# Splitting the first product of a recurrent mixer into uneven parts of k tiles

## The chip, the cores and the metric

The kernel runs on one core of one Trainium2 chip. The metric is the device time in microseconds (us) of one execution. Engines are named as the profile names them: PE is TensorE's matmul, PEld its weight load, DVE is VectorE, ACT is ScalarE, POOL is GpSimd, and SP is SyncE, which issues the loads.

## The reference

256 tokens of width 1024 pass through two blocks. The first has a mixer of gated linear attention (GLA) and retention, and then a mixture of 32 experts with 2 chosen per token. The second has an HGRN2 mixer, a convolutional feed-forward net, a latent attention and a second net. The change lies in the HGRN2 mixer and reaches back into the experts ahead of it:

```
def _hgrn2_mixer(h, w_in, lower_bound, out_norm, w_out):
    q, f, i, g = jnp.split(h @ w_in, 4, axis=-1)          # w_in: 1024 x 4096
    forget = lb + (1.0 - lb) * jax.nn.sigmoid(f)
    key_in, log_f = 1.0 - forget, jnp.log(forget)
    o = _chunk_gated_recurrence(heads(jax.nn.silu(q)), heads(key_in), heads(i), heads(log_f))   # 8 heads of 128
    o = _rmsnorm_2(o, out_norm) * jax.nn.silu(heads(g))
    return o.reshape(B, S, D_MODEL) @ w_out
```

Everything is float32. Ahead of the mixer stand the experts' second product (hidden times `wd`, weighted and summed into the residual) and two norms in a row.

## The kernel before, in words

SBUF beside the constants is a pool of 21 equal tiles "S" of 128 x 2048 words. A weight chunk is one load of 1 MiB into one such tile. `add` puts the chunks into one stream, in which they are loaded in order by SP; `prefetch` issues as many loads as a plan, made from a dry run of the same program, says will fit. A chunk that a float32 product needs with full precision is split by `split` into a high and a low part (4 ACT copies into `wh`, 4 DVE subtractions into `wl`, two more S tiles), and `mm3` makes one product of three matmuls of those parts. `get` also splits the chunk that follows. The framework's scheduler puts the instructions of each engine into a fixed order from the program's order and a model of costs; each engine then runs its own list in that order. PSUM has 8 banks.

The experts' second product (in `moe`) runs over 64 blocks i: each takes a chunk `ex_d` of 1 MiB, makes 32 small matmuls into a bank `y` (L1165), ACT copies the bank (L1169), and 2 matmuls with `ct` sum it into `cb` (L1177). Eight blocks fill one k tile (128 of 1024 features) of the mixer's input, so `hgrn_tile(k)` comes at block i = 8k + 9 and transposes and scales that tile (L1320).

The mixer's first product is 1024 x 4096: 8 k tiles times 8 groups of 512 columns. Groups 0 and 2 are the forget gates f of heads 0 to 3 and 4 to 7, groups 1 and 3 the queries q, 4 and 5 the values, 6 and 7 the output gates. It is done in four parts p of two k tiles each (2p, 2p + 1), a part being 4 chunks `hg_in` of two groups. Parts 0 to 2 are "fillers": generators that `tick` advances by one step of one k tile and one group (12 matmuls of 256 columns or 6 of 512) behind each block. Part 0 is queued at tile 1, so its ticks run in blocks 17 to 32; part 1 in 33 to 48; part 2 from 49 to the end. Sums over the parts are kept in four S tiles `hsum`, one for two groups: part 0 is copied there by ACT (L1381), parts 1 and 2 are added by DVE (L1383). The chunks of parts 0 to 2 stand in the stream before `ex_d` chunks 12, 16, 20, ... 56, and their `split` is called at those blocks.

Part 3 (k tiles 6 and 7) runs in `hgrn`, after the experts. There the sum of the earlier parts first enters the PSUM bank by a matmul with the identity (L1356), then 24 more matmuls follow, and the result is read straight from PSUM: for f and q by a multiplication with the norm's row (L1440, DVE), for values and gates by an activation with the norm's column as scale (L1456, ACT). The norm's scale comes from the filler `close` (POOL L448, row by L506).

For each half c (4 heads), `prep(c)` turns f and q into decays and keys, then `decay_levels` runs seven doubling steps of DVE multiplications (L575, L576, L578) and small PE products (L546 `sc`, L553 to L562 `sd`); it holds four banks `sc` until step 16 and two banks `sd` until the scores are read. `decay_scores` sums six levels per head by matmuls with the identity (L604, `cd`), masks them (L611) and copies the far parts; `decay_out` multiplies by the values (L633 to L635), takes the norm over each head, and scales. `gate(c)` multiplies by the gates (L1503) and transposes (L520). `out_proj` then has two halves: the first needs `gate(0)`, the second `gate(1)`.

The order before: chunk 12 (f and q of half 0), `prep(0)`, then chunks 13 (f and q of half 1), 14 (values), 15 (gates) with the filler `chains` at one tick per k tile and group (six steps of half 0's levels, then both halves in turn); `prep(1)` comes behind chunk 13; `decay_out` of half 1 is queued behind all that as a filler of `out_proj`, four ticks per chunk.

`decay_scores` is called three times: once for the GLA mixer of the first block and twice here.

Of the kernel before, what the change touches and what calls it, by code (L numbers as in the profile page):

```python
# [19 lines left out]
P = 128  # L20
T = 256
D = 1024
# [71 lines left out]
def _layout(z):  # L94
# [9 lines left out]
    def pairs(a):  # L104
# [20 lines left out]
    out["hg_in"] = np.ascontiguousarray(  # L125
        hw.reshape(4, 2, P, 4, 2, 512).transpose(0, 3, 2, 4, 1, 5).reshape(16, P, 2048))
# [34 lines left out]


# [61 lines left out]
class Kern:  # L224
# [371 lines left out]
    def decay_scores(self, sc):  # L596

        nc = self.nc
        bm = self.c("bmask").rearrange("p (b i) -> p b i", b=4)[:, None].to_broadcast([P, 2, 4, 32])
        cd = self.bank("cd")  # L600
        for h in range(4):
            tv = sc["tm"][:, h * 384:(h + 1) * 384].rearrange("p (t l i) -> p t l i", t=2, l=6)
            for l in range(6):
                nc.tensor.matmul(cd[:, h * 64:(h + 1) * 64].rearrange("p (t i) -> p t i", t=2), self.ident, tv[:, :, l],  # L604
                                 start=h == 0 and l == 0, stop=h == 3 and l == 5)
        yield
        for h in range(4):
            st = sc["st"][:, h * 384:(h + 1) * 384]
            stv = st.rearrange("p (t i) -> p t i", t=3)
            b2 = sc["b2"][h // 2][:, h % 2 * 256:(h % 2 + 1) * 256]  # L610
            nc.vector.tensor_mul(stv[:, 0:3:2].rearrange("p t (b i) -> p t b i", b=4),  # L611
                                 cd[:, h * 64:(h + 1) * 64].rearrange("p (t i) -> p t i", t=2)[:, :, None, :]
                                 .to_broadcast([P, 2, 4, 32]), bm)
            nc.scalar.copy(st[:, 128:256], b2[:, 0:128])
            for t in range(2):
                d = st[:, 256 * t:256 * t + 128]
                nc.scalar.copy(d[0:64, 64:128], b2[64 * t:64 * t + 64, 128:192])
                for b in range(2):
                    nc.scalar.copy(d[64 * b:64 * b + 32, 64 * b + 32:64 * b + 64],
                                   b2[64 * b + 32 * t:64 * b + 32 * t + 32, 192:224])  # L620
            yield
# [53 lines left out]
    def setup(self):  # L675
# [22 lines left out]
        for r in range(16):  # L698
            if 3 <= r < 15:
                self.add(("hg_in", r - 3), A["hg_in"][r - 3], True)  # L700
            for i in range(4 * r, 4 * r + 4):
                self.add(("ed", i), A["ex_d"][i], False)
# [303 lines left out]
    def moe(self):  # L1006
# [149 lines left out]
        for i in range(64 + 2):  # L1156
            if i < 64:
                if i % 4 == 0 and 12 <= i < 60:
                    self.split(("hg_in", i // 4 - 3))
# [155 lines left out]
    def hgrn_tile(self, k):  # L1315

        nc, x, n = self.nc, self.x, self.hn
        b = self.bank("tp")
        for t in range(2):
            nc.tensor.transpose(b[:, t * P:(t + 1) * P], x[:, t * D + k * P:t * D + (k + 1) * P], self.ident)  # L1320
        self.high_low(b, self.hw[:, k:k + 1], n["h"], n["l"], k * T)
        if k % 2:
            self.fillers.append(self.hgrn_part(k // 2))
            if k < 7:
                self.hgrn_squares(k // 2)
# [16 lines left out]
    def hgrn_part(self, p, only=None, evict=None):  # L1342

        nc, n = self.nc, self.hn
        for s in range(4) if only is None else (only,):
            key = ("hg_in", 4 * p + s)
            h, l = self.get_split(key) if p < 3 else self.get(key)
            if p == 0:
                self.hsum[s] = self.S("hsum")
            for gi in range(2):  # L1350
                outs = [self.bank("gf") for _ in range(2)]
                sums = [self.hsum[s][:, o:o + 512] for o in ((gi * 1024, gi * 1024 + 512) if s < 2 else
                                                             (gi * 512, D + gi * 512))]
                if evict:
                    for a, b in zip(sums, outs):
                        nc.tensor.matmul(b, self.ident, a, start=True, stop=False)  # L1356
                for q in range(2):
                    o = (2 * p + q) * T
                    w = slice(gi * 1024 + q * 512, gi * 1024 + (q + 1) * 512)
                    first = q == 0 and not evict  # L1360
                    if s < 2:
                        xh, xl = n["h"][:, o:o + T], n["l"][:, o:o + T]
                        for ft in range(4):
                            a = slice(w.start + ft * P, w.start + (ft + 1) * P)
                            self.mm3(outs[ft // 2][:, (ft % 2) * T:(ft % 2 + 1) * T], h[:, a], l[:, a], xh, xl,
                                     first and ft % 2 == 0, q == 1 and ft % 2 == 1)
                    else:
                        for t in range(2):
                            a = slice(o + t * P, o + (t + 1) * P)
                            self.mm3(outs[t], n["h"][:, a], n["l"][:, a], h[:, w], l[:, w], first, q == 1)  # L1370
                    if q == 0:
                        yield
                if gi:
                    self.free(h, l)
                if evict:
                    evict(gi, sums, outs)
                    if gi and s < 2:
                        self.free(self.hsum[s])
                for a, b in zip(sums, outs):
                    if p == 0:  # L1380
                        nc.scalar.copy(a, b)  # L1381
                    elif p < 3:
# [3 lines left out]
    def hgrn(self):  # L1386
# [10 lines left out]
        self.fillers.pop()  # L1397
# [4 lines left out]

        def part(s, evict, ticks):
            for _ in self.hgrn_part(3, s, evict):
                self.tick(ticks)

        def close():
# [13 lines left out]
            yield  # L1421
# [5 lines left out]
            yield  # L1427
# [6 lines left out]
        def ev_row(dst):  # L1434
            def f(gi, sums, outs):
                if rowb is None:
                    late.append((f, (gi, sums, outs)))
                    return
                for i, o in enumerate(outs):
                    nc.vector.tensor_mul(e2(dst[gi][:, 1024 + i * 512:1536 + i * 512]), e2(o), rowb)  # L1440
            return f
# [10 lines left out]

        def ev_tok(func):
            def f(gi, sums, outs):
                for t, o in enumerate(outs):
                    nc.scalar.activation(sums[t], o, func, scale=rs[:, t:t + 1])  # L1456
            return f
# [13 lines left out]
        g = self.hsum[3]  # L1471
        self.fillers.append(close())
        part(0, ev_row((fr[0], kq[0])), 1)
        self.drain()
        prep(0, fr[0], kq[0])
# [11 lines left out]

        self.fillers.append(chains())
        part(1, ev_row((fr[1], kq[1])), 1)
        prep(1, fr[1], kq[1])  # L1490
        part(2, ev_tok(AF.Copy), 1)
        part(3, ev_tok(AF.Silu), 1)
# [3 lines left out]
        self.fillers.append(self.decay_out(sc[1], v, 4, P))  # L1496
# [376 lines left out]
```

## Time and profile before

| what | value |
|---|---|
| median of 3 runs | 1508.77 us (1504.38 to 1510.76) |
| the profiled execution, its own time | 1510.53 us |
| its span in the trace | 1508.5 us |
| PE busy | 1362.1 us, 90% of the span |
| DVE busy, ACT busy | 781.2 us, 649.4 us |
| loads | 368.31 MB on SP's queue |

All times in the rows below are microseconds from the start of the span. The own time holds 2.0 us that lie outside the span. A busy PE is a PE that has matmuls under way; they are pipelined, so a group "x48" with its total length tells more than the length of one record. A float32 matmul leaves two records in the trace.

### The profile page before, as it was taken

To read this page: it belongs to the slowest core of one execution; us is meant where nothing else is said; L and a number is where in the kernel's file an instruction comes from. 1 tells how busy PE (TensorE), PEld (TensorE's weight loads), DVE (VectorE), ACT (ScalarE), POOL (GpSimd) and SP (SyncE) were. 2 spreads that over 40 slices of the span, in tenths; PEclk is the share of its full clock that TensorE was granted. 3 is DMA by queue.
4 is the path that set the end of the run, shared out by engine and by line. 5 is a ranking of instruction groups with operands and counts; after the bars stand their busy time and mean duration, and the time that the engine had idled before them with its cause. 6 is when DMAs were issued, how large, how long until landed. Compare 5 with 4: busy or idle time off the path is not lost.

```text
span 1508.5 us, 28797 instructions
## 1 busy us (share of the span) xinstructions
PE 1362.1 (90%) x12062; PEld 1103.4 (73%) x12062; DVE 781.2 (52%) x1685; ACT 649.4 (43%) x1489; POOL 22.3 (1%) x25
## 2 busy tenths in 40 slices
PE   7999999999897666766699998889999998999998
PEld 6799878877763243324588876679999976899997
DVE  4876376645510020000124438548777767687794
ACT  5564535733310010000243326447566576565672
POOL 0000000000000000000000000000000010000000
PEclk9999999999898788768899999989999999999999
DMA  8353623485899999999999990536453215565400
GB/s 337 153 196 113 223 84 140 142 348 200 369 374 420 420 419 421 421 421 420 420 388 359 417 404 30 197 115 248 168 196 113 77 46 206 210 213 196 164 1 28
DMA packets 53544, 370.20 MB, mean 245 GB/s; under 512 B 6161, under 2 KB 7057, under 8 KB 9634
## 3 DMA queue, kind: packets, MB, share of 16 engines
q1 hardware_dynamic: 53410, 368.31, 62.3%
q8 instruction: 96, 1.57, 0.4%
q14 instruction: 38, 0.31, 0.1%
HBM read 367.24 MB, written 1.05 MB: 244 GB/s over the span
## 4 chain that ended last, share of the span: by engine, by line
PE 68%; DMA 22%; ACT 4%; DVE 4%; issue 1%; POOL 1%; SPq 0%; POOLq 0%; ACTq 0%; DVEq 0%
DMA w<-in_ex_gu 16%; PE u L370 6%; PE u L372 6%; PE u L371 6%; DMA w<-in_ex_d 5%; PE gt L371 5%; PE gt L372 5%; PE gt L370 5%; PE gf L370 3%; PE gf L371 3%; PE gf L372 3%; PE acc L371 3%; PE acc L370 3%; PE acc L372 3%; PE y L1165 3%; PE cb L1177 1%
## 5 line engine op out<-in xcount | busy, mean ns | idle before, releaser
L322 DVE TENSOR_TENSOR wl<-w,wh 128x512 fp32r<-128x512 f32 (+2 forms) x644 | 400.6, 666 | 106.1 <-ACT wh L321 84.0
L321 ACT ACTIVATE wh<-w 128x512 fp32r<-128x512 f32 (+2 forms) x644 | 348.0, 612 | 151.1 <-PE u L371 61.9
L1274 PE MATMUL gu<-w,t 128*32 128x256 f32 x2048 | 161.5, 457 | 51.6 <-DMA w<-in_ex_gu 51.3
L370 PE MATMUL u<-xh,wh 128*128 128x256 f32 x704 | 199.4, 283 | 0.0
L371 PE MATMUL u<-xl,wh 128*128 128x256 f32 x704 | 199.2, 283 | 0.0
L372 PE MATMUL u<-xh,wl 128*128 128x256 f32 x704 | 199.0, 283 | 0.0
L1274 PEld LDWEIGHTS gu<-w,t 128*32 128x32 f32 x2048 | 65.1, 124 | 130.8 <-DMA w<-in_ex_gu 80.7
L370 PEld LDWEIGHTS u<-xh,wh 128*128 128x128 f32 x704 | 134.9, 192 | 0.9
L371 PEld LDWEIGHTS u<-xl,wh 128*128 128x128 f32 x704 | 134.9, 192 | 0.7
L372 PEld LDWEIGHTS u<-xh,wl 128*128 128x128 f32 x704 | 134.9, 192 | 0.0
L1278 DVE TENSOR_TENSOR t<-t,gu 128x128 f32<-128x128 f32 x32 | 9.2, 288 | 209.5 <-ACT t L1277 209.5
L370 PE MATMUL gt<-wh,xh 128*128 128x512 f32 (+1 forms) x288 | 112.9, 392 | 0.0
L1277 ACT ACTIVATE t<-gu 128x128 f32<-128x128 f32 x32 | 8.9, 278 | 237.6 <-PE gu L1274 237.6
L372 PE MATMUL gt<-wh,xl 128*128 128x512 f32 (+1 forms) x288 | 109.7, 381 | 0.0
L371 PE MATMUL gt<-wl,xh 128*128 128x512 f32 (+1 forms) x288 | 109.5, 380 | 0.0
L370 PE MATMUL gf<-xh,wh 128*128 128x256 f32 x320 | 95.7, 299 | 3.0 <-ACT wh L321 3.0
L372 PE MATMUL gf<-xh,wl 128*128 128x256 f32 x320 | 92.4, 291 | 0.0
L371 PE MATMUL gf<-xl,wh 128*128 128x256 f32 x320 | 91.8, 287 | 0.0
L1165 PE MATMUL y<-w,ht 128*32 128x128 f32 x2048 | 72.3, 283 | 10.6 <-DMA w<-in_ex_d 9.9
L1566 DVE SCALAR_TENSOR_TENSOR t<-t,prm,t 128x254 f32<-128x254 f32 (+1 forms) x176 | 74.3, 478 | 2.7 <-ACT t L1564 2.3
L1169 ACT COPY t<-y 128x128 f32<-128x128 f32 x64 | 17.0, 268 | 133.7 <-PE y L1165 133.7
L1165 PEld LDWEIGHTS y<-w,ht 128*32 128x32 f32 x2048 | 55.2, 113 | 21.8 <-issue 13.4
(414 smaller groups left out, 2346.0 us busy)
## 6 DMA issues: line engine op xcount, KB each, us to landing
w<-in_ex_gu SPq DMA_DIRECT2D x128, 1024.0 KB, 19.8
w<-in_ex_d SPq DMA_DIRECT2D x64, 1024.0 KB, 10.5
w<-in_w_in SPq DMA_DIRECT2D x44, 1024.0 KB, 4.9
w<-in_f_up SPq DMA_DIRECT2D x44, 1024.0 KB, 4.8
w<-in_f_dn SPq DMA_DIRECT2D x22, 1024.0 KB, 4.8
w<-in_hg_in SPq DMA_DIRECT2D x16, 1024.0 KB, 11.1
w<-in_br_ret SPq DMA_DIRECT2D x8, 1024.0 KB, 8.8
w<-in_br_gla SPq DMA_DIRECT2D x4, 1024.0 KB, 5.7
```

Of the source, the lines that this page charges most:

```text
L321: self.nc.scalar.activation(h[:, a], r[:, a], AF.Copy)
L322: self.nc.vector.tensor_sub(l[:, a], r[:, a], h[:, a].bitcast(F32))
L370: mm(out, lh, rh, start=first, stop=False)
L371: mm(out, lh, rl, start=False, stop=False)
L372: mm(out, ll, rh, start=False, stop=last)
L1165: mm(b[32 * e:32 * e + 32, 0:P], ht[o // 2048][:, o % 2048:o % 2048 + 32], w[:, e * 512 + j * P:e * 512 + (j + 1) * P], start=j == 0, stop ...
L1169: nc.scalar.copy(Ys[i], b[:, 0:P])
L1177: mm(acc[k][:, t * P:(t + 1) * P], cts[:, g * T + t * P:g * T + (t + 1) * P], Y, start=g == 0 and t == 0, stop=g == 7 and t == 1)
L1274: nc.tensor.matmul(b[32 * j:32 * j + 32, 0:256], xg[k // 4][:, (k % 4) * P + 32 * e:(k % 4) * P + 32 * e + 32], w[:, o:o + 256], start=k = ...
L1277: nc.scalar.activation(sg, b[:, 0:128], AF.Silu)
L1278: nc.vector.tensor_mul(hd, sg, b[:, 128:256])
L1566: nc.vector.scalar_tensor_tensor(ys[:, j:], us[:, :T - j], cw[:, 3 * c + 2 - j:3 * c + 3 - j], ys[:, j:], op0=ALU.mult, op1=ALU.add)
```

## The change

The parts become uneven: k tile 0; 1 and 2; 3 and 4; 5 and 6 (of these last only f and q ahead of the mixer). `HG_SLOTS` says which k tiles and groups each of the 16 chunks holds, `HG_PART` at which tile which chunks are queued, `HG_AT` before which block a chunk is loaded and split: the first two move from 12 and 16 to 4 and 8, the other ten stay. The fillers run in blocks 9 to 16 (k tile 0), 25 to 40, 41 to 56, and 57 to the end. The mixer keeps four chunks: k tile 7 for f and q of both halves, then tiles 5 to 7 for values and gates. For values and gates the earlier sum is no longer brought in by an identity matmul; DVE adds PSUM to `hsum` and ACT applies the scale from there. Both `prep` follow the first chunk; `chains` runs beside the values and gates; `decay_out` of half 1 is issued before `gate(0)`. `decay_scores` uses 6 matmuls of 256 columns in place of 24 of 64.

```diff
+HG_SLOTS = ([((0,), (0, 1, 2, 3)), ((0,), (4, 5, 6, 7))] +
+            [((k, k + 1), (g, g + 1)) for k in (1, 3) for g in (0, 2, 4, 6)] +
+            [((5, 6), (0, 1)), ((5, 6), (2, 3)), ((7,), (0, 1, 2, 3)), ((5, 6), (4, 5)), ((7,), (4, 5, 6, 7)),
+             ((5, 6), (6, 7))])
+HG_PART = {0: range(0, 2), 2: range(2, 6), 4: range(6, 10), 6: range(10, 12)}
+HG_AT = {i: n for n, i in enumerate((4, 8, 20, 24, 28, 32, 36, 40, 44, 48, 52, 56))}
...
-        for h in range(4):
-            tv = sc["tm"][:, h * 384:(h + 1) * 384].rearrange("p (t l i) -> p t l i", t=2, l=6)
-            for l in range(6):
-                nc.tensor.matmul(cd[:, h * 64:(h + 1) * 64].rearrange("p (t i) -> p t i", t=2), self.ident, tv[:, :, l],
-                                 start=h == 0 and l == 0, stop=h == 3 and l == 5)
+        tv = sc["tm"][:, 0:1536].rearrange("p (z l i) -> p z l i", z=8, l=6)
+        for l in range(6):
+            nc.tensor.matmul(cd[:, 0:256].rearrange("p (z i) -> p z i", z=8), self.ident, tv[:, :, l], start=l == 0,
+                             stop=l == 5)
...
-                if i % 4 == 0 and 12 <= i < 60:
-                    self.split(("hg_in", i // 4 - 3))
+                if i in HG_AT:
+                    self.split(("hg_in", HG_AT[i]))
...
-        if k % 2:
-            self.fillers.append(self.hgrn_part(k // 2))
-            if k < 7:
-                self.hgrn_squares(k // 2)
+        if k in HG_PART:
+            self.fillers.append(self.hgrn_part(HG_PART[k]))
+        if k % 2 and k < 7:
+            self.hgrn_squares(k // 2)
...
+    def hgrn_part(self, slots):
+        nc = self.nc
+        for i in slots:
+            ks, gs = HG_SLOTS[i]
+            h, l = self.get_split(("hg_in", i))
+            for j, g in enumerate(gs):
+                outs = [self.bank("gf") for _ in range(2)]
+                for q, k in enumerate(ks):
+                    self.hgrn_mm(outs, g, k, h, l, (j * len(ks) + q) * 512, q == 0, q == len(ks) - 1)
+                    if q < len(ks) - 1:
+                        yield
+                if g == gs[-1]:
+                    self.free(h, l)
+                if ks == (0,) and g % 2 == 0:
+                    self.hsum[g // 2] = self.S("hsum")
+                for a, b in zip(self.hgrn_sums(g), outs):
+                    if ks == (0,):
+                        nc.scalar.copy(a, b)
+                    else:
+                        nc.vector.tensor_add(a, a, b)
+                yield
...
-        part(0, ev_row((fr[0], kq[0])), 1)
+        h, l = self.get(("hg_in", 12))
+        for gi in range(4):
+            outs = [self.bank("gf") for _ in range(2)]
+            for a, b in zip(self.hgrn_sums(gi), outs):
+                nc.tensor.matmul(b, self.ident, a, start=True, stop=False)
+            self.hgrn_mm(outs, gi, 7, h, l, gi * 512, False, True)
+            ev_row(gi, outs)
+            self.tick()
+        self.free(h, l)
         self.drain()
-        prep(0, fr[0], kq[0])
+        self.free(*self.hsum[0:2])
+        for c in range(2):
+            prep(c, fr[c], kq[c])
...
         self.fillers.append(chains())
-        part(1, ev_row((fr[1], kq[1])), 1)
-        prep(1, fr[1], kq[1])
-        part(2, ev_tok(AF.Copy), 1)
-        part(3, ev_tok(AF.Silu), 1)
+        w7 = None
+        for gi in range(4, 8):
+            if gi % 2 == 0:
+                w5 = self.get(("hg_in", 13 if gi == 4 else 15))
+            w7 = w7 or self.get(("hg_in", 14))
+            outs = [self.bank("gf") for _ in range(2)]
+            for k in (5, 6, 7):
+                w, o = (w7, (gi - 4) * 512) if k == 7 else (w5, (gi % 2 * 2 + k - 5) * 512)
+                self.hgrn_mm(outs, gi, k, *w, o, k == 5, k == 7)
+                self.tick()
+            if gi % 2:
+                self.free(*w5)
+            for t, (a, b) in enumerate(zip(self.hgrn_sums(gi), outs)):
+                nc.vector.tensor_add(a, a, b)
+                nc.scalar.activation(a, a, AF.Copy if gi < 6 else AF.Silu, scale=rs[:, t:t + 1])
+        self.free(*w7)
...
-        self.fillers.append(self.decay_out(sc[1], v, 4, P))
+        self.now(self.decay_out(sc[1], v, 4, P))
```

`hgrn_mm` (new) makes the products of one k tile and one group, the same matmuls as before. In `close`, two of its four pauses go.

## Rows read from the trace of the kernel before

**Rows 1.** Busy time by stretch: bounds, length, busy us (instructions) of each engine, clock, DMA, GB/s

```profile
719.40:745.50 26.10, 17.88 (x292) 13.82 (x290) 0.57 (x2) 3.41 (x13) 0.00 (x0) 0.81 1.01 420
745.50:778.00 32.50, 30.59 (x433) 26.50 (x432) 10.76 (x20) 14.64 (x35) 0.00 (x0) 0.94 0.99 396
...
901.00:910.00 9.00, 4.81 (x19) 2.55 (x19) 4.75 (x24) 6.62 (x16) 1.39 (x2) 0.99 0.36 148
910.00:924.00 14.00, 12.09 (x78) 10.37 (x76) 10.04 (x17) 10.94 (x17) 0.00 (x0) 0.88 0.00 1
924.00:939.00 15.00, 14.74 (x368) 10.61 (x368) 13.72 (x22) 10.32 (x18) 0.00 (x0) 1.00 0.21 73
939.00:954.00 15.00, 14.66 (x410) 10.88 (x409) 13.66 (x26) 6.09 (x10) 0.00 (x0) 1.00 0.16 53
954.00:978.70 24.70, 18.57 (x270) 15.41 (x269) 12.12 (x34) 10.56 (x52) 2.02 (x2) 0.92 0.68 266
978.70:1001.80 23.10, 23.07 (x128) 20.18 (x128) 8.51 (x18) 11.76 (x50) 0.00 (x0) 0.86 0.21 72
1001.80:1010.00 8.20, 2.00 (x10) 1.58 (x9) 5.31 (x17) 6.12 (x23) 2.01 (x2) 0.72 0.76 321
```

**Rows 2.** Instructions in order of time, PE: the transposes of tiles 0, 1, 2, 7

```profile
719.36 0.38 PE L1320 MATMUL tp<-ident,xn 128*128 128x128 f32 x2
745.51 0.63 PE L1320 MATMUL tp<-ident,xn 128*128 128x128 f32 x2
775.17 0.38 PE L1320 MATMUL tp<-ident,xn 128*128 128x128 f32 x2
900.94 0.44 PE L1320 MATMUL tp<-ident,xn 128*128 128x128 f32 x2 [0.67 <-DVE xn L1181]
```

**Rows 3.** The same view, PE: one block without a filler

```profile
707.89 1.08 PE L1165 MATMUL y<-w,ht 128*32 128x128 f32 x32 [0.32 <-DMA w<-in_ex_d]
709.40 0.71 PE L1177 MATMUL cb<-t,ct 128*128 128x128 f32 x4 [0.43 <-ACT t L1169]
```

**Rows 4.** The same view: the first mixer chunk's load, split and product

```profile
705.33 0.33 SPq L307 DMA_DIRECT2D w<-in_hg_in  x1
748.24 2.17 ACT L321 ACTIVATE wh<-w 128x512 fp32r<-128x512 f32 x4
748.90 0.39 PE L370 MATMUL gf<-xh,wh 128*128 128x256 f32 x1 [1.85 <-ACT wh L321]
```

**Rows 5.** The same view, PE: the three level sums

```profile
78.07 5.46 PE L604 MATMUL cd<-tm,ident 128*128 128x64 f32 x48
953.47 5.57 PE L604 MATMUL cd<-tm,ident 128*128 128x64 f32 x48
988.24 5.47 PE L604 MATMUL cd<-tm,ident 128*128 128x64 f32 x48
```

**Rows 6.** The same view, PE: two identity matmuls of 512 columns

```profile
937.55 1.88 PE L1356 MATMUL gf<-hsum,ident 128*128 128x512 f32 x4
```

**Rows 7.** One line's instructions, DVE: ns min/median/max, first and last start

```profile
L1383 DVE TENSOR_TENSOR hsum<-hsum,gf x32: 677/687/689, 807.0 to 899.9; 128x512 f32<-128x512 f32 x32
```

**Rows 8.** Instructions in order of time: marks of the mixer's chain

```profile
923.75 1.21 DVE L565 TENSOR_TENSOR hfr<-hkq,hfr 128x1024 f32<-128x1024 f32 x1
939.26 1.22 DVE L565 TENSOR_TENSOR hfr<-hkq,hfr 128x1024 f32<-128x1024 f32 x1
974.16 0.68 DVE L576 TENSOR_TENSOR hfr<-hfr 128x512 f32<-128x512 f32 x1
980.59 0.80 PE L370 MATMUL op<-wh,oh 128*128 128x512 f32 x1
1008.11 2.14 PE L520 MATMUL tp<-ident,hsum 128*128 128x128 f32 x8 [6.20 <-DVE hsum L1503]
1009.91 0.77 PE L370 MATMUL op<-wh,oh 128*128 128x512 f32 x1
```

**Rows 9.** The page's 40 slices of 37.7 us: busy tenths of PE

```profile
PE   7999999999897666766699998889999998999998
```

More of the change, by code (lines that the diff above doesn't have):

```diff
@@ L124, in _layout @@
     hw = np.stack([hw[:, c, h] for c, h in ((1, 0), (0, 0), (1, 1), (0, 1), (2, 0), (2, 1), (3, 0), (3, 1))], axis=1)
-    out["hg_in"] = np.ascontiguousarray(
-        hw.reshape(4, 2, P, 4, 2, 512).transpose(0, 3, 2, 4, 1, 5).reshape(16, P, 2048))
+    hw = hw.reshape(8, P, 8, 512)
+    out["hg_in"] = np.stack([np.stack([hw[k, :, g] for g in gs for k in ks], axis=1).reshape(P, 2048)
+                             for ks, gs in HG_SLOTS])
     out["hg_out"] = _chunks(f["hgrn_w_out_2"][0], k_first=True)
@@ L697, in setup @@
                 self.add(("gu", e, i), A["ex_gu"][e, i], False)
[L698 to L702, printed above, removed]
+        for i in range(64):
+            if i in HG_AT:
+                self.add(("hg_in", HG_AT[i]), A["hg_in"][HG_AT[i]], True)
+            self.add(("ed", i), A["ex_d"][i], False)
         for n, o, m in (("hg_in", 12, 16), ("hg_out", 0, 4)):
@@ L1157, in moe @@
             if i < 64:
-                if i % 4 == 0 and 12 <= i < 60:
-                    self.split(("hg_in", i // 4 - 3))
+                if i in HG_AT:
+                    self.split(("hg_in", HG_AT[i]))
                 w = self.get(("ed", i))
@@ L1340, in hgrn_squares @@
                 self.square_sum(self.hss[:, o:o + 1], x[:, a])
[L1342 to L1350, printed above, removed]
-                outs = [self.bank("gf") for _ in range(2)]
[L1352 to L1366, printed above, removed]
-                    else:
[L1368 to L1382, printed above, removed]
@@ new lines, in hgrn_sums, with hgrn_mm @@
+    def hgrn_sums(self, g):
+        s = self.hsum[g // 2]
+        return [s[:, o:o + 512] for o in ((g % 2 * 1024, g % 2 * 1024 + 512) if g < 4 else
+                                          (g % 2 * 512, D + g % 2 * 512))]
+    def hgrn_mm(self, outs, g, k, h, l, o, first, last):
+        n = self.hn
+        if g < 4:
+            xh, xl = n["h"][:, k * T:(k + 1) * T], n["l"][:, k * T:(k + 1) * T]
+            for ft in range(4):
+                a = slice(o + ft * P, o + (ft + 1) * P)
+                self.mm3(outs[ft // 2][:, (ft % 2) * T:(ft % 2 + 1) * T], h[:, a], l[:, a], xh, xl,
+                         first and ft % 2 == 0, last and ft % 2 == 1)
+        else:
+            for t in range(2):
+                a = slice(k * T + t * P, k * T + (t + 1) * P)
+                self.mm3(outs[t], n["h"][:, a], n["l"][:, a], h[:, o:o + 512], l[:, o:o + 512], first, last)
@@ L1396, in hgrn @@
         nc.vector.tensor_scalar(om, lb, -1.0, 1.0, op0=ALU.mult, op1=ALU.add)
-        self.fillers.pop()
         n = self.hn
@@ L1401, in hgrn @@
         late = []
-        def part(s, evict, ticks):
-            for _ in self.hgrn_part(3, s, evict):
-                self.tick(ticks)
         def close():
@@ L1420, in close @@
             yield
-            yield
             rowb = self.row_of(rs)[:, None, :].to_broadcast([P, 2, T])
@@ L1426, in close @@
                 f(*a)
-            yield
         def e2(a):
@@ L1432, in hgrn, with ev_row @@
         sc = [{}, {}]
[L1434 to L1441, printed above, removed]
+        def ev_row(g, outs):
+            if rowb is None:
+                late.append((ev_row, (g, outs)))
+                return
+            dst = (fr, kq)[g % 2][g // 2]
+            for i, o in enumerate(outs):
+                nc.vector.tensor_mul(e2(dst[:, 1024 + i * 512:1536 + i * 512]), e2(o), rowb)
         def prep(c, fr, kq):
@@ L1451, in prep @@
             nc.scalar.activation(k, F, AF.Identity, bias=1.0, scale=-1.0)
[L1453 to L1457, printed above, removed]
         def both(*gens):
```

## Prediction

> **What bounds the kernel now.** I read the tenths of the page first: PE stands at 6 to 9 nearly everywhere [rows 9], so a change pays where PE or a chain that ends at PE is late. Then the stretches of the experts' second product and of the mixer [rows 1]. The reader should see three regimes. Up to tile 1 (719.4 to 745.5) PE is busy 17.9 of 26.1 us while the loads run at 420 GB/s: the loads set the pace, 1.0486 MB / 420 GB/s = 2.5 us for a chunk. From 745.5 on the fillers run; PE is busy 30.6 of 32.5 us and the loads fall to 396 GB/s: PE sets the pace, the loads wait for tiles. After the last tile, 901 to 1010, hardly a load matters; PE is busy 4.8 + 12.1 + 14.7 + 14.7 + 18.6 + 23.1 + 2.0 = 90.0 us of 109.0, idle 19.0, and DVE 4.8 + 10.0 + 13.7 + 13.7 + 12.1 + 8.5 + 5.3 = 68.1 us. Last I followed the mixer's chain in order of time [rows 5, 8]: levels of half 0 begin at 923.75, of half 1 at 939.26, their last step stands at 974.16; the output product starts at 980.59, the scores of half 1 are summed only at 988.24, and the second half of the output product waits for them until 1009.91, with 6.2 us of idle PE just before. The sum below is made against the profiled execution's own 1510.5 us, which is 1.8 us above the median of 1508.77.
>
> **Level sums.** Each call has 24 matmuls, 48 records, in 5.5 us: 0.114 us a record for 64 columns [rows 5]. After it there are 12 records of 256 columns. No row shows that form. From above: a record of 512 columns costs 1.88 / 4 = 0.47 us [rows 6], 12 of them 5.6 us, no gain. From below: if a record costs no more than one of 64 columns, 12 x 0.114 = 1.4 us. A record of 512 columns costs four times one of 64 with eight times the columns, so columns bind at that end, and I take half of 0.47, 0.235 us: 12 x 0.235 = 2.8 us, a gain of 2.65 us a call (0 to 4.1). The three calls stand at 78, 953 and 988 us. At 78, in the third slice, PE is full [rows 9], so 2.65 us come off there; the other two belong to the mixer. Of the weight loads the Trainium skill ("TensorE: Matmul & The Clock Gate", section LDWEIGHTS) says that one takes its columns over 1.2 GHz, 107 ns for 128; the 114 ns of the row agree. If that alone bound the new form too, a call would fall to 12 x 107 ns = 1.3 us and the whole forecast by 3 x 1.5 = 4.6 us, to 1483.
>
> **The experts' second product.** The count of fillers is the same, 48 steps of one k tile and group; eight of them (k tile 0) move from behind tile 1 to behind tile 0, where PE is idle a third of the time. Two chunks pass twelve `ex_d` chunks less in SP's queue: by block 17 twenty chunks are needed before and after, so block 17 still lands near 742.6, but tile 0 comes two loads, 5.0 us, later, at 724.4 instead of 719.4 [rows 2]. Eight blocks with a filler took 775.2 - 745.5 = 29.7 us [rows 2], splits and evictions included, so block 17 is reached by PE at 754. Eight blocks without a filler need 1.08 + 0.71 = 1.8 us each on PE [rows 3], 14.3 us, to 768.4; the loads for blocks 18 to 25 are ten chunks, 25 us from 742.6, 767.6, and with the block's own 1.9 us tile 2 stands at 769.5. Before it stood at 775.2: 5.7 us earlier. From there on nothing differs: five stretches in (900.9 - 775.2) / 5 = 25.15 us each against ten loads, 25.0 us. These two paces are so close that there is little stock of loaded chunks, and I count 5 us kept. Bounds: 0, if the stock runs out as often as PE saved; 15, if PE kept the loads' pace to the end (8 x (29.7 - 14.3) / 8 = 15.4 us of fillers are moved out).
> The evictions of k tile 0 remain 16 ACT copies. DVE's adds grow from 32 to 40 here, 8 x 0.69 = 5.5 us [rows 7], hidden under a DVE that is idle for most of the stretch (10.8 of 32.5 us busy [rows 1]); without that cover, 5.5 us. The four sum tiles are taken some eight blocks earlier out of the 21; the loads have 25 us for ten chunks at that place, and I cost it at nothing, with the 0 above as its bound.
>
> **The mixer behind the experts.** The product itself is the same 16 steps. Eight identity matmuls go (values and gates), 8 x 0.94 = 7.5 us of PE [rows 6], and two level sums shrink by 5.3: PE's work falls from 90.0 to 77.2 us. DVE gets 8 adds, 5.5 us [rows 7], 73.6 in all. Neither is 109, so what ends is the chain, step by step:
> - Half 0 starts its levels near 923: its groups still come first, and the wait for the norm is as before. Half 1 is ready some 10 us earlier than 939.26, since both `prep` follow one chunk, but it needs the four banks that half 0 holds until its sixth step.
> - Half 0's levels ran from 923.75 to the level sum at 953.47. Between two steps PE had up to 1.9 us of identity matmuls [rows 6] and a product step; some five such pairs stood in that time, and without them, and with the shorter sum behind it, I expect about 942 to 945.
> - Half 1's levels took 974.8 - 939.3 = 35.6 us, 8 of them behind the 5.6 us level sum and two identity pairs. I expect 27 us from about 938: 965.
> - From half 0's level sum to the first output product were 980.6 - 953.5 = 27.1 us, now less 2.65: about 969. Its first half took at most 1001.8 - 980.6 - 5.5 = 15.7 us beside the level sum [rows 1, 5, 8], so it ends by 985.
> - From half 1's level sum to the second half were 1009.9 - 988.2 = 21.7 us, now 19; the sum starts at 965 instead of waiting behind the output product: 984.
> So the second half could start at 984 to 985 instead of 1010. Against these 26 us I set the adds on DVE (5.5 us) and, as an estimate without a row, as much again for the two halves' chains meeting on ACT, DVE and POOL: 15 us kept. Bounds: 5.3 us (only the level sums lie on the chain) and 26 us.
> The waits that this adds: an add waits for its product, and behind it on DVE stand the level steps, for which PE's small products wait; each is a wait of one product step, at most the (29.7 - 14.3) / 8 = 1.9 us that a filler costs a block, eight times, 15 us in all, and that would bring the lower of the two bounds.
>
> **Sum.** 1510.5 - 2.65 - 5 - 15 = 1487.9 against the own time; the runs' median lies 1.8 lower, of which I take half: 1487.
>
> **The rivals.**
> 1. DVE becomes the bound in the mixer. For it: between 924 and 954 DVE is already busy 27.4 of 30 us, and it gets the adds. Against it: it idles half of 954 to 978.7 [rows 1]. Then the chain keeps only the level sums: 1510.5 - 2.65 - 5 - 5.3 = 1497.5.
> 2. The experts' stretch gives nothing, since its end follows the loads. For it: 25.15 against 25.0 us. Against it: the loads stood at 396 GB/s right behind tile 1, so PE, not they, was late. 1510.5 - 2.65 - 15 = 1492.9.
> 3. Slower: the first split is late. Its load was issued at 705.3 and ACT reached its split only at 748.2, when PE had waited 1.85 us for it [rows 4]; the order of ACT's list is the scheduler's choice. If the split stays where it was, PE, which runs its list in order, holds the products behind tile 0 and all blocks after them from 724 on; each microsecond from about 726 moves tile 2 by one, for there is no slack left (768.4 against 767.6). With the first product at 748.9 as before, 22 us are lost, which cancels the rest: 1487 + 22 = 1509; from 756 on the kernel is slower by over 0.5%. Against it: before, the split stood right ahead of its first use, so it should move with it.
> 4. The change does what it says, but the halves' chains do not disturb each other: 1510.5 - 2.65 - 5 - 26 = 1477.
>
> **Chances.** Forecast (1480 to 1493) 0.50; rival 1 0.20 (1493 to 1504); rival 2 0.12; rival 3 0.08, half of it over 1516; rival 4 0.10. A measurement of this kernel tells about 0.5%, 7.5 us, from no change: 1501.2 to 1516.3 is "same". Faster: 0.50 + 0.12 + 0.10 + 0.13 of rival 1 = 0.85; same: 0.07 of rival 1 and 0.03 of rival 3 = 0.10; slower 0.05. The range runs from rival 4's side, 1475, over rivals 1 and 2 to 1502, which leaves out rival 3 and the end of rival 1, about 0.14.
>
> **What would show it.** Level sums: groups of 12 records near 2.8 us. Experts: tile 0 near 724, the first product of the mixer right behind it, tile 2 near 769, tile 7 near 896, loads at 420 GB/s through the blocks without fillers. Mixer: 8 identity matmuls in all; the last level step less than 68 us behind tile 7 instead of 73; the level sum of half 1 ahead of the first output product; second half of the output product some 94 us behind tile 7 instead of 109, without 6 us of idle PE ahead of it. The prediction is wrong if tile 7 does not come earlier, if ACT's first split stands near 748, or if DVE is full from 924 to 975 and the levels end as late as before.

## The result, and the profile after

The changed kernel takes 1492.38 us (median of 4 runs, 1491.45 to 1493.10), beside 1509.09 us for the kernel before on the same chip: a ratio of 0.9894, 95% interval 0.9871 to 0.9917. The profiled execution took 1491.84 us (span 1489.8) where that of before took 1510.53, so 18.7 us went where 22.65 were forecast; the medians differ by 16.7.

Executions of one kernel differ by some us already in their first stages, so marks are compared by the distance between them. Three are enough: the reciprocal square root `rsy` of the linear attention's norm on POOL (102.13 before, 99.91 after, behind the first level sum), the transposes of tile 7 (900.94 and 893.45), and the feed-forward's first product `u` (1023.71 and 1005.03). From `rsy` to tile 7, where the experts lie, it was 798.8 us and is 793.5; from tile 7 to `u`, the mixer's tail, 122.8 and 111.6. So 5.3 us came from the experts' stretch, 11.2 from the tail and 2.2 from what lies ahead of `rsy`. Of the kernel before, two of the marks:

```profile
102.13 1.39 POOL L448 TENSOR_TENSOR rsy<-rsm,mhalf 128x4 f32<-128x4 f32 x1 [76.34 <-DVE rsm L442]
1023.71 0.36 PE L370 MATMUL u<-xh,wh 128*128 128x256 f32 x1
```

Instructions of the changed kernel in order of time: start us, us, engine, line, tiles, count, and in brackets the idle time before it and who ended it. The line numbers have moved: L613 is L604 of before, L1328 L1320, L575, L585, L586 and L588 the level steps, L1470 the identity matmuls, L1506 the new adds, L1519 the gates, L530 their transposes.

```profile
78.62 2.75 PE L613 MATMUL cd<-tm,ident 128*128 128x256 f32 x12
99.91 1.39 POOL L458 TENSOR_TENSOR rsy<-rsm,mhalf 128x4 f32<-128x4 f32 x1 [73.68 <-DVE rsm L452]
...
723.04 4.27 ACT L331 ACTIVATE wh<-w 128x512 fp32r<-128x512 f32 x8
723.64 0.63 PE L1328 MATMUL tp<-ident,xn 128*128 128x128 f32 x2
727.73 0.79 PE L380 MATMUL gf<-xh,wh 128*128 128x256 f32 x2 [2.96 <-ACT xh L481]
755.45 0.38 PE L1328 MATMUL tp<-ident,xn 128*128 128x128 f32 x2
769.34 0.38 PE L1328 MATMUL tp<-ident,xn 128*128 128x128 f32 x2
...
893.45 0.44 PE L1328 MATMUL tp<-ident,xn 128*128 128x128 f32 x2 [0.67 <-DVE xn L1189]
893.72 1.88 PE L1470 MATMUL gf<-hsum,ident 128*128 128x512 f32 x4
895.88 3.60 PE L1470 MATMUL gf<-hsum,ident 128*128 128x512 f32 x8
902.04 1.19 PE L516 MATMUL rw<-ident,hrs 128*128 128x128 f32 x4 [2.56 <-DVE hrs L1419]
908.28 1.88 PE L1470 MATMUL gf<-hsum,ident 128*128 128x512 f32 x4
913.55 1.23 DVE L575 TENSOR_TENSOR hfr<-hkq,hfr 128x1024 f32<-128x1024 f32 x1
916.80 0.69 DVE L586 TENSOR_TENSOR hfr<-hfr 128x512 f32<-128x512 f32 x1
919.74 4.30 DVE L332 TENSOR_TENSOR wl<-w,wh 128x512 fp32r<-128x512 f32 x7
923.96 0.68 DVE L585 TENSOR_TENSOR hkq<-hkq,hfr 128x512 f32<-128x512 f32 x1
925.30 0.95 PE L556 MATMUL sc<-hfr,hkq 128*32 128x32 f32 x64 [2.26 <-DVE hfr L586]
...
947.03 2.86 PE L613 MATMUL cd<-tm,ident 128*128 128x256 f32 x12
962.53 1.03 PE L613 MATMUL cd<-tm,ident 128*128 128x256 f32 x4
963.04 0.68 DVE L586 TENSOR_TENSOR hfr<-hfr 128x512 f32<-128x512 f32 x1
964.78 1.89 PE L613 MATMUL cd<-tm,ident 128*128 128x256 f32 x8
966.98 1.29 DVE L1519 TENSOR_TENSOR hsum<-hsum,hsum 128x512 f32<-128x512 f32 x2 [0.95 <-ACT hsum L652]
969.16 0.49 PE L642 MATMUL o<-hsum,st 128*128 128x128 f32 x2 [2.49 <-ACT st L628]
973.95 1.04 PE L530 MATMUL tp<-ident,hsum 128*128 128x128 f32 x8
977.36 0.50 PE L380 MATMUL op<-wh,oh 128*128 128x512 f32 x1 [2.38 <-ACT hsum L652]
979.89 1.29 DVE L1519 TENSOR_TENSOR hsum<-hsum,hsum 128x512 f32<-128x512 f32 x2 [0.55 <-ACT hsum L652]
989.27 1.04 PE L530 MATMUL tp<-ident,hsum 128*128 128x128 f32 x8
991.83 0.51 PE L380 MATMUL op<-wh,oh 128*128 128x512 f32 x1 [1.52 <-ACT wh L331]
...
1005.03 0.36 PE L380 MATMUL u<-xh,wh 128*128 128x256 f32 x1
```

The reader is to see four things. A level sum takes 2.75 to 2.92 us (half 1's, in two pieces, 1.03 and 1.89) instead of 5.5 [rows 5]. The first split stands at tile 0, and tile 2 comes at 769.3 instead of 775.2 [rows 2, 4]. Half 1's level sum now runs ahead of the output product and no longer among the matmuls of its first half. And half 0's second level step (923.96) stands behind 4.3 us of weight splits on DVE, with PE waiting 2.26 us for it.

Busy time of the engines in the changed kernel: bounds, length, busy us (instructions) of PE, PEld, DVE, ACT and POOL, granted clock, DMA share, GB/s. The second line is the stretch of the levels.

```profile
893.50:902.50 9.00, 6.44 (x20) 3.25 (x21) 4.74 (x24) 6.62 (x16) 1.39 (x2) 0.96 0.06 24
902.50:946.50 44.00, 38.46 (x763) 30.21 (x766) 41.19 (x69) 27.49 (x44) 0.00 (x0) 0.89 0.04 8
```

The same 44 us, 9 us behind tile 7, in the kernel before:

```profile
910.00:954.00 44.00, 41.49 (x855) 31.87 (x853) 37.42 (x63) 27.35 (x43) 0.00 (x0) 0.96 0.13 43
```

PE was 94% busy there and DVE 85%; now DVE is 94% busy and PE 87%, at a granted clock of 0.89 instead of 0.96. The bound of this stretch has changed engines.

### The profile page after: what moved, and what is told of

Its sections match the earlier page's. It is cut to its first block, busy times and chain, and to the rows that moved or that the text cites. A ratio compares the mean times of both kernels' runs of the same rounds, so it can differ in the third digit from the quotient of the medians.

```text
span 1489.8 us, 28565 instructions
## 1 busy us (share of the span) xinstructions
PE 1349.7 (91%) x11938; PEld 1091.6 (73%) x11938; DVE 790.7 (53%) x1701; ACT 650.3 (44%) x1489; POOL 22.3 (1%) x25
## 4 chain that ended last, share of the span: by engine, by line
PE 69%; DMA 20%; DVE 5%; ACT 4%; issue 1%; POOL 1%; SPq 0%; POOLq 0%; ACTq 0%; DVEq 0%
DMA w<-in_ex_gu 16%; PE u L380 6%; PE u L381 6%; PE u L382 6%; PE gt L381 5%; PE gt L382 5%; PE gt L380 5%; PE y L1173 3%; PE gf L380 3%; PE gf L381 3%; PE gf L382 3%; PE acc L381 3%; PE acc L380 3%; PE acc L382 3%; DMA w<-in_ex_d 3%; PE cb L1185 2%
## 5 line engine op out<-in xcount | busy, mean ns | idle before, releaser
L332 DVE TENSOR_TENSOR wl<-w,wh 128x512 fp32r<-128x512 f32 (+2 forms) x644 | 399.9, 666 | 87.3 <-ACT wh L331 69.8
L381 PE MATMUL acc<-wl,t 128*128 128x512 f32 x176 | 70.2, 399 | 0.0
```

The lines of the kernel that those rows point to most:

```text
L332: self.nc.vector.tensor_sub(l[:, a], r[:, a], h[:, a].bitcast(F32))
L381: mm(out, lh, rl, start=False, stop=False)
```

## The experiments

"From tile 7" columns are distances from its transposes, in the profiled execution of each kernel; the medians are of all its runs, and the ratio goes by runs of the kernel before on the same chip (medians 1507.70 to 1509.09). Each edit is told below.

| kernel | median us | ratio to before, 95% | `rsy` to tile 7 | last level step from tile 7 | `u` from tile 7 |
|---|---|---|---|---|---|
| before | 1509.09 | | 798.8 | 73.2 | 122.8 |
| the change | 1492.38 | 0.9894 (0.9871 to 0.9917) | 793.5 | 69.6 | 111.6 |
| old sums | 1501.46 | 0.9945 (0.9929 to 0.9961) | 794.6 | 71.8 | 116.4 |
| before with the new sums | 1502.34 | 0.9959 (0.9947 to 0.9972) | 803.8 | 70.9 | 117.4 |
| first part late | 1499.31 | 0.9939 (0.9922 to 0.9957) | 799.1 | 69.0 | 112.2 |
| scores as filler | 1496.12 | 0.9912 (0.9897 to 0.9927) | 794.9 | 69.8 | 115.7 |
| gate first | 1491.09 | 0.9889 (0.9874 to 0.9904) | 793.2 | 69.0 | 111.4 |
| gate in the middle | 1494.48 | 0.9912 (0.9900 to 0.9925) | 793.9 | 69.7 | 114.8 |
| identities | 1490.82 | 0.9882 (0.9867 to 0.9897) | 792.9 | 67.5 | 110.7 |
| middle and identities | 1491.58 | 0.9887 (0.9872 to 0.9901) | 795.4 | 67.5 | 111.5 |
| adds twice | 1498.52 | 0.9933 (0.9917 to 0.9949) | 792.8 | 76.0 | 119.9 |
| split early | 1491.65 | 0.9886 (0.9866 to 0.9906) | 795.3 | 67.4 | 110.8 |
| split early, identities | 1491.04 | 0.9885 (0.9865 to 0.9904) | 793.3 | 67.1 | 110.4 |

**Level sums.** Two kernels: the change with the old 24 matmuls, and the kernel before with the new 6.

```diff
+        for h in range(4):
+            tv = sc["tm"][:, h * 384:(h + 1) * 384].rearrange("p (t l i) -> p t l i", t=2, l=6)
...
-        tv = sc["tm"][:, 0:1536].rearrange("p (z l i) -> p z l i", z=8, l=6)
```

> The changed kernel with the 24 narrow level sums of the kernel before in all three calls. Theory: each call stands on the path that sets the end, so each costs 5.5 - 2.8 = 2.7 us: the GLA norm's step on POOL moves from 99.9 back to about 102, and the two calls of the mixer add about 5 us more: some 1499 to 1500 us against 1492. Rival: in the mixer PE idles beside the DVE steps, so the two calls there are hidden and only the first one's 2.2 us come back: 1494 to 1495.

> The kernel before with the six wide level sums alone. Theory: in the changed kernel the three calls were worth 2.8 (GLA) and 4.9 us (mixer); in the kernel before, the calls of the mixer stand on the path as well, the second of them alone on PE with the whole chain of half 1 behind it: 2.7 + 5 = 7 to 8 us, 1501 to 1502 us against 1509. Rival: there the PE is so full beside them that other work moves into the space: only the GLA call and one more count, 1504.

With the old sums the tail is 4.9 us longer and the median 9.1 us higher; the new sums alone take 5.4 us off the tail and off the median of the kernel before (1507.70 beside it), less than the 7 to 8 us expected. The two sums of the mixer are 5.3 us shorter, and the tail shows about 5 of it in both kernels, so both lie on the path. What the sum in the linear attention gives can't be read from the medians better than as 0 to 4 us, but the traces tell it. From the start of that sum to `rsy` it is 24.06 us before (78.07 to 102.13) and 24.07 in the change with the old sums (79.46 to 103.53); in all eleven traces with the new ones it is 21.29 to 21.31. So this sum lies on the path to `rsy` too, with 2.8 us.

**The first part's place.** The first two chunks go back to blocks 12 and 16 and their part to tile 1, all else as in the change.

```diff
-HG_PART = {0: range(0, 2), 2: range(2, 6), 4: range(6, 10), 6: range(10, 12)}
-HG_AT = {i: n for n, i in enumerate((4, 8, 20, 24, 28, 32, 36, 40, 44, 48, 52, 56))}
+HG_PART = {1: range(0, 2), 2: range(2, 6), 4: range(6, 10), 6: range(10, 12)}
+HG_AT = {i: n for n, i in enumerate((12, 16, 20, 24, 28, 32, 36, 40, 44, 48, 52, 56))}
```

> The changed kernel with k tile 0's products queued at tile 1 (blocks 17 to 24) and its two chunks before blocks 12 and 16, as the first part was before. Theory: eight filler steps go back from the stretch that waits for loads to the one that PE paces; tile 2 comes at about 775 instead of 769.3, tile 7 5 to 6 us later than 893.5, and the whole at 1497 to 1498. Rival: the loads set the end of that stretch and the early steps were free either way: tile 7 within 1 us of 893.5, the whole at 1492.

Tiles 0, 1, 2 and 7 of that kernel, in order of time:

```profile
716.28 0.38 PE L1328 MATMUL tp<-ident,xn 128*128 128x128 f32 x2
742.43 0.63 PE L1328 MATMUL tp<-ident,xn 128*128 128x128 f32 x2
773.99 0.38 PE L1328 MATMUL tp<-ident,xn 128*128 128x128 f32 x2
...
898.04 0.44 PE L1328 MATMUL tp<-ident,xn 128*128 128x128 f32 x2 [0.67 <-DVE xn L1189]
```

From tile 0 to tile 2 it is 57.7 us here, 55.8 before, 45.7 after. With the late place the stretch from `rsy` to tile 7 is 799.1 us again, and the median is 6.9 us higher than the change's. Up to tile 2 the loss is 5.7 us (675.1 us from `rsy` against 669.4); behind it, tile 2 to tile 7, this kernel takes the change's 124.1 us and not the 125.8 of before. In the ten profiled kernels with the early place the stretch is 792.8 to 795.4 us, in the three with the late one 798.8 to 803.8; the 5 us between the two executions of the unchanged stretch (before, and before with the new sums) show how far one execution may be off. The rival, by which the loads set the end whatever PE does, falls.

**The order behind the levels.** First, half 1's scores go back into the output product as a filler.

```diff
-        self.now(self.decay_out(sc[1], v, 4, P))
+        self.fillers.append(self.decay_out(sc[1], v, 4, P))
```

> The changed kernel with the scores and outputs of half 1 queued as a filler of the output product again, as before. Theory: most of what the mixer gained beyond the level sums comes from this order; here half 1's level sum waits behind the first 24 output matmuls, the second half of the output product starts 4 to 8 us later than 991.8, the whole at 1496 to 1500. Rival: the order gives with one hand and takes with the other, since in the changed kernel half 0's transposes wait on PE behind half 1's products (ready at 968.3, run at 974.0); then this run is within 2 us of 1492 or faster.

PE in that kernel, in order of time:

```profile
968.85 1.26 PE L530 MATMUL tp<-ident,hsum 128*128 128x128 f32 x8 [3.03 <-DVE hsum L1519]
...
977.53 2.75 PE L613 MATMUL cd<-tm,ident 128*128 128x256 f32 x12
...
994.67 2.14 PE L530 MATMUL tp<-ident,hsum 128*128 128x128 f32 x8 [6.22 <-DVE hsum L1519]
```

Half 1's sum (977.53) falls back among the output product, and 6.2 us of idle PE stand ahead of the second transposes again, as before [rows 8]. It costs 4.1 us of tail and 3.7 of median, the low end of what the theory allowed: the gates' transposes for half 0 (968.85, 74.7 us behind tile 7 against 80.5 in the change) come earlier in exchange.

Can both be had? Two kernels try it: `gate(0)` issued ahead of half 1's scores; and, on top, `gate(1)` issued inside the output product's first half, before its last 24 matmuls.

```diff
-        self.now(self.decay_out(sc[1], v, 4, P))
...
         gate(0)
+        self.now(self.decay_out(sc[1], v, 4, P))
...
-            if kh and mid:
-                mid()
             for c in range(2):
+                if mid and not kh and c:
+                    mid()
```

(The last hunk belongs to the second kernel alone.)

> The changed kernel with the gate and transposes of half 0 issued ahead of the scores and outputs of half 1. Theory: half 0's transposes, ready at 968.3 and run at 974.0 behind half 1's products, start some 5 us earlier, and the output product with them; the second half of it then waits for half 1 instead, so 2 to 5 us are gained in all: 1487 to 1490 against 1492. Rival: half 1's chain is the longer one, and each product that goes ahead of it delays the end: 1492 to 1494.

> The one before and, beside it, the gate and transposes of half 1 issued ahead of the last 24 matmuls of the output product's first half instead of behind them. Theory: where half 1's transposes stood behind PE's full list (ready at 981.2, run at 989.3) the 2.5 us of idle PE behind them go: 1 to 3 us better than the run before. Rival: half 1 is not ready by then, PE runs its list in order and waits with work behind it: 0 to 4 us worse than the run before.

The first, PE in order of time:

```profile
966.30 1.06 PE L530 MATMUL tp<-ident,hsum 128*128 128x128 f32 x4 [2.79 <-DVE hsum L1518]
...
972.68 0.49 PE L642 MATMUL o<-hsum,st 128*128 128x128 f32 x2 [1.02 <-ACT st L628]
...
988.25 1.03 PE L530 MATMUL tp<-ident,hsum 128*128 128x128 f32 x8
```

Half 0's transposes come 6.8 us earlier (73.7 us behind tile 7), but PE waits 2.8 us for them ahead of half 1's products, and the second transposes stand 95.6 us behind tile 7 against 95.8: nothing is won there, and my theory falls (1491.09 us lies between its range and the rival's). In the second kernel PE reaches the second transposes before half 1 is gated:

```profile
978.99 0.47 PE L380 MATMUL op<-wh,oh 128*128 128x512 f32 x1
986.22 0.33 PE L530 MATMUL tp<-ident,hsum 128*128 128x128 f32 x1 [1.52 <-DVE hsum L1518]
1007.09 0.66 PE L492 MATMUL tp<-ident,xn 128*128 128x128 f32 x4 [1.99 <-DVE xn L445]
```

and the tail is 3.3 us longer. The matmuls of the output product behind this transpose waited with it. The Trainium skill ("TensorE: Matmul & The Clock Gate", section "Step-by-step: what each phase is for") says that PE pulls weight loads ahead and keeps matmuls in program order; the row agrees. But this wait does not explain the 3.3 us: the 1.52 us that PE waits in the change behind the second transposes (991.83), for weight splits on ACT, are gone in exchange. Two other differences stand in the trace: the output product starts 86.3 us behind tile 7 instead of 83.9, and PE waits 1.99 us for DVE ahead of the last transposes before `u` (1007.09), a wait that the change does not show. What caused these two stays open.

**Which engine sets the levels' pace.** Values and gates brought in by eight identity matmuls again, instead of the eight adds on DVE:

```diff
+            for a, b in zip(self.hgrn_sums(gi), outs):
+                nc.tensor.matmul(b, self.ident, a, start=True, stop=False)
...
-                nc.vector.tensor_add(a, a, b)
-                nc.scalar.activation(a, a, AF.Copy if gi < 6 else AF.Silu, scale=rs[:, t:t + 1])
+                nc.scalar.activation(a, b, AF.Copy if gi < 6 else AF.Silu, scale=rs[:, t:t + 1])
```

> The changed kernel with the earlier sums of values and gates brought in by eight identity matmuls on PE again, in place of eight DVE adds; ACT reads PSUM. Theory: from 902 to 946 DVE is 94% busy and sets the levels' pace, so giving it back 5.5 us and loading PE with 7.5 us costs nothing or gains: the last level step ends 0 to 4 us earlier than 963.7, the whole at 1488 to 1493. Rival, as the prediction counted it: PE's work sets the pace, and the whole is 5 to 7.5 us longer, 1497 to 1500.

The 44 us of the levels in that kernel, 9 us behind tile 7:

```profile
899.30:943.30 44.00, 42.99 (x839) 31.77 (x839) 38.74 (x65) 27.00 (x44) 0.00 (x0) 0.97 0.05 16
```

PE is full (43.0 of 44 us) in place of DVE, the levels end 2.1 us earlier, `u` comes 0.8 us earlier and the median is 1.6 us lower, less than the intervals can part. The other way round, each add issued twice, the second into a spare tile:

```diff
+                nc.vector.tensor_add(self.t512(), a, b)
                 nc.vector.tensor_add(a, a, b)
```

> The changed kernel with each of the eight adds for values and gates issued a second time into a spare tile, so that DVE has eight operations of 0.68 us, 5.4 us, more beside the levels and no other engine anything. Theory (DVE, 94 per cent busy from 902 to 946, sets the pace): the last level step comes 3 to 5.4 us later than 69.6 us behind tile 7, and tile 7 to the feed-forward's first product grows from 111.6 by 2 to 5 us. Rival (PE's own order sets the pace and DVE has room): under 1 us on both.

Its last level step on DVE:

```profile
970.06 0.68 DVE L586 TENSOR_TENSOR hfr<-hfr 128x512 f32<-128x512 f32 x1
```

It stands 76.0 us behind tile 7. The engines while its levels run:

```profile
902.50:946.50 44.00, 34.16 (x738) 26.61 (x739) 40.90 (x69) 24.52 (x39) 0.00 (x0) 0.88 0.01 2
946.50:970.00 23.50, 19.71 (x299) 15.95 (x299) 15.98 (x34) 10.81 (x45) 1.01 (x1) 0.72 0.72 275
```

Eight operations of 0.68 us, 5.4 us, move the last level step by 6.4 us, `u` by 8.3 and the median by 6.1. DVE has no room in the change. The step and the tail moved by more than the theory's 5.4 and 5 us; in the second stretch the granted clock is 0.72 where the change had 0.92 in the corresponding one (946.5 to 967), so a PE that waits for DVE is then also slower at what it does, which I take for the surplus but did not isolate.

Three more kernels take work off the levels. `gate(1)` in the middle together with the identities:

> Both changes of order and the identity matmuls for values and gates in place of DVE's adds. Theory: DVE sets the levels' pace, so the identity matmuls let the levels end 2 us earlier, and with half 1's transposes no longer late this reaches the end: 1 to 3 us better than the run before, 1483 to 1487. Rival: PE has become the bound behind the levels, and 7.5 us more of it cost 1 to 4 us.

This is 2.9 us below the middle alone, as the theory wanted, but its 1483 to 1487 us are missed, and the median is only 0.8 us below the change's, which the intervals can't part. Next, chunk 12 is loaded and split before block 60, so that its splits (ACT 900.63 to 904.88, DVE to 906.7 in the change) leave the stretch behind the norm; alone and with the identities.

```diff
-HG_AT = {i: n for n, i in enumerate((4, 8, 20, 24, 28, 32, 36, 40, 44, 48, 52, 56))}
+HG_AT = {i: n for n, i in enumerate((4, 8, 20, 24, 28, 32, 36, 40, 44, 48, 52, 56, 60))}
...
-        h, l = self.get(("hg_in", 12))
+        h, l = self.get_split(("hg_in", 12))
+        self._split_to(self.pos[("hg_in", 13)])
```

> The changed kernel, with the mixer's first remaining chunk (k tile 7, f and q of both halves) loaded and split before block 60 of the experts' second product instead of behind its end. In the changed kernel ACT copies the high parts of two chunks from 900.63 to 904.88 and DVE the low parts from 901.81 to 906.7, behind the wait for the norm, in which PE idles 2.56 us up to 902.04; the products of k tile 7 begin at 902.88. Theory (DVE sets the pace of the levels, and what it is spared there comes back in part): the products move into the wait, DVE has 2.5 us less to do behind 902, tile 7 to the feed-forward's first product falls by 2 to 4 us from 111.6, median 1488 to 1491. Rival (the end is set by the order of PE behind the levels): under 1 us, median 1491.5 to 1493. If the split disturbs the experts' last blocks, tile 7 comes later against the chunks' start (793 us from the linear attention's norm) by up to 2.5 us.

> The early split together with values and gates brought in by identity matmuls instead of DVE adds. Theory: with 2.5 us of splits and 5.5 us of adds less on DVE, and PE filled in the wait, tile 7 to the feed-forward's first product is 107 to 109.5 us and the median 1487 to 1490, below both single edits. Rival (PE is full as soon as the identities are back, or the order of PE behind the levels decides): no better than the better of the two single edits, 1490 to 1492.

Both theories fall. The levels end 2.2 and 2.5 us earlier than in the change, `u` comes only 0.8 and 1.2 us earlier, and the medians (1491.65, 1491.04) lie with those of the change and of the identities. In both, the mixer's norm also came later: its `rsy` stands 7.9 us behind tile 7 instead of 4.5, which may have taken back part of what the split was to give. No version tried here beats the change by more than the measurement can tell.

## Why the prediction was right, and where it was not

The forecast was 1487 and the time is 1492.4, inside the likeliest case's 1480 to 1493, by 0.6 us. Against the profiled execution's 1491.8 us, rival 2's sum, 1492.9, lies nearer than the forecast's 1487.9, so the total does not part the two; the marks do. Point by point:

- **Level sums.** Right. 12 records take 2.75 to 2.92 us against 2.8 forecast, 0.23 to 0.24 us a record against 0.235, and all three are shown on the path: 2.8 us up to `rsy`, about 5 of the tail. By the Trainium skill's rule for weight loads ("TensorE: Matmul & The Clock Gate", section LDWEIGHTS), columns over 1.2 GHz, a call bound by them alone would by an estimate fall to 1.3 us. It did not: 2.75 / 12 = 0.229 us a record is half the 0.47 of 512 columns, so the 256 columns bind here.
- **The experts' stretch.** Right in the sum, 5.3 us against 5, but in part by luck. Tiles 0, 2 and 7 stand at 723.6, 769.3 and 893.5 against 724, 769 and 896, but these marks hold the 2.2 us from ahead of `rsy`, which the forecast of the marks had left out. Counted from `rsy`, tile 0 came 6.5 us later (forecast 5.0) and tile 2 came 3.6 us earlier (forecast 5.7). PE waited 2.96 us for the first product, so block 17 was reached at 755.5 and not 754; the eight blocks behind it took PE 13.9 us, with no idle time between 755.5 and 769.3, so that PE and not a late load set tile 2. The other 1.7 us came between tiles 2 and 7, where the prediction has "From there on nothing differs": 125.8 us before and 124.1 after, 125.8 again in the kernel before with the new sums, and between 124 and 125 in all eleven kernels with the uneven parts. What PE waited for there, before and after (us in total, times, longest):

```profile
PE cb L1177 <- ACT t L1169: 4.0, 7, 1.4
PE cb L1185 <- ACT t L1177: 2.3, 6, 0.4
```

ACT copied the first part's sums from 766.4 to 802.1 us before, on both sides of tile 2; the 1.4 us wait falls into that time. In the change the last of these copies starts at 754.0. This is the likely source of the 1.7 us, which no run isolated. Rivals 2 and 3 fall.
- **The mixer's tail.** The mechanism was right, the size was not: 11.2 us against 15. The step that failed is "without them, and with the shorter sum behind it, I expect about 942 to 945" for half 0's level sum, 41 to 44 us behind tile 7. It stands 53.6 us behind it; before it was 52.5. Its levels start earlier than before (20.1 us behind tile 7 against 22.8), but half 1's `prep`, the splits and the adds now come between its steps on DVE. Taking out the identity matmuls, costed at 7.5 us of PE against 5.5 us on DVE, only moved the full engine from PE to DVE: putting them back costs nothing and gains, if anything, about 1 us (0.8 of tail). Of the eight identities that remain, six run in the wait for the norm, where they cost nothing: 2.56 us of idle PE still follow them.
- **What follows from it.** The first output product was forecast 68 us behind tile 7 and came 83.9 behind (before 79.7): half 0's gated values are ready at 968.3, but its transposes stand behind half 1's products on PE until 973.95. The second half of the output product was to come some 94 us behind tile 7 and came 98.4 behind (before 109.0). The last level step was to be under 68 us behind tile 7 and is 69.6.
- **The rivals.** Rival 1 is true in its mechanism and not in its price: DVE is the bound while the levels run, yet the tail kept 11.2 us and not only the 5.3 of the sums, since the order of half 1's scores gives 4.1 of its own. Rival 4 falls: the two halves' chains do disturb each other.

The account of the tail: 4.9 us level sums, 4.1 us half 1's scores ahead of the output product, and 2.2 us left over, with both `prep` early and the identities gone, less about 0.8 that the exchange costs. The parts were measured one at a time, and that they add up was not shown. What lies ahead of `rsy` gave 2.2 us: the level sum's 2.8, less 0.6 by which the execution of the change was behind already when that sum began (78.62 against 78.07).

## What to carry to other kernels

Where two engines are each 85% busy or more in one stretch, moving work from one to the other may move the bound and not the end, as here: read busy time in the stretch itself before an exchange is costed as a gain. A step that is brought forward in one engine's order pushes back all that stood behind it; forecast the new order of the whole chain, mark by mark from a common event, not only the piece that was late. And matmuls with few columns are worth merging where they stand on the path, even when the engine looks full of other work.

## What the runs showed of the hardware

- A float32 matmul's record costs 0.114 us at 64 columns [rows 5], 0.23 at 256 and 0.47 at 512 [rows 6]: between 64 and 256 columns four times the columns cost twice the time.
- A wait on PE can be paid twice. With the scores as filler, half 1's 8 transposes take 2.14 us behind 6.22 us of idle PE, at a granted clock of 0.50, which is 1.2 of 2.4 GHz; half 0's take 1.04 in the changed kernel, with no wait right ahead of them, at 1.00. Not every wait costs that: half 0's with the scores as filler take 1.26 us behind 3.03 us of idle PE, at 1.00. With the adds doubled the clock is 0.72 while the levels end. The three stretches in this order; the third number from the right is the granted clock:

```profile
994.60:996.80 2.20, 2.13 (x9) 1.82 (x10) 2.20 (x6) 1.60 (x5) 0.00 (x0) 0.50 0.00 0
973.90:975.00 1.10, 1.08 (x10) 0.84 (x9) 0.17 (x1) 1.10 (x10) 0.15 (x1) 1.00 1.00 425
968.80:970.20 1.40, 1.26 (x8) 0.84 (x8) 0.60 (x1) 0.38 (x2) 0.00 (x0) 1.00 0.58 240
```

- Executions of unchanged stages differ: the experts' stretch by 5 us between two executions, the stage ahead of `rsy` by 4 (97.4 to 101.3 us over the traces with the new sums), though from the level sum's start to `rsy` they agree within 0.02 us. A single profile locates a gain of that size, and only the comparison with several others makes it safe.
